# The last two attention heads: output-weight tiles and turned rows prepared at earlier steps, filling products taken weight tile by weight tile

## The chip, the core and the metric

The kernel runs on one core of a Trainium2 chip. The core has five engines, each with its own queue of instructions, which it works through in order: TensorE (PE; its weight loads are shown as PEld), VectorE (DVE), ScalarE (ACT), GpSimd (POOL) and SyncE (SP), which here issues all transfers. They meet only at semaphores. PE writes to PSUM, which has eight banks of 128 x 512 numbers; ACT and DVE read them.

The metric is the time of one execution on the device in microseconds (us). Three runs of the kernel before took 1289.68, 1290.79 and 1286.98 us; the median is 1289.68.

## What is computed

One decoder layer on 1024 tokens of width 1024, in float32. Only the first half matters here:

```python
h = rmsnorm(x, mix_pre_norm)
q_a, k_a, v_a, q_h, f_h, i_h, g_h = split(h @ w_in)
attn = dilated_mixture_attention(q_a, k_a, v_a)     # 8 heads of 64
attn = rmsnorm(attn, attn_out_norm)                  # 512 columns
rec = hgrn2_recurrence(q_h, f_h, i_h, g_h)           # 512 columns
mixed = concatenate([attn, rec]) @ w_out
x = x + rmsnorm(mixed, mix_post_norm)
x = x + rmsnorm(relu(rmsnorm(x, mlp_pre_norm) @ w_ff1)**2 @ w_ff2, mlp_post_norm)
```

The recurrence `rec` is ready before the attention begins, so its part of the product with `w_out` can be made while the attention runs. The attention norm is one factor per token, so it can be applied to the product afterwards.

## The kernel before

**Precision.** Every operand of a large product is split into a high and a low part: ACT copies it to the rounded format (L83), DVE takes the remainder (L84). A product is then three matmuls, high x high, low x high and high x low (`three_pass`, L87 to L89). With 512 columns that is one *unit* in what follows: one 128-row slice of weights times one token tile.

**The order is written by hand.** The instructions stand on each engine in the order in which the program records them. Two devices shape it. `queue` holds generators that emit filling work in small pieces, and `fill(ns)` lets them emit until the pieces' nominal costs have used up the given budget (a piece of 650 is one unit); a generator that yields `None` is not ready and ends the filling. `drain()` empties the queue.

**The attention loop** has 64 steps, `s = 8 * head + block`, each for 128 queries. Step `s` records: the exponentials of step s+1 on ACT (`expo`, L681); the scores of step s+2, two matmuls for each 512 keys (`score`, L667 and L668, into banks "s") with bias and maximum on DVE (L670); the transposes of its own exponentials (`turn`, L694), four to a bank "t", split by ACT (L697) and DVE (L698); for each pair of blocks the products with the values (`weigh`, L711, copied by ACT to `ot`, L714), whose result is turned back a step later (`finish`, L722), reduced by DVE (L726) and multiplied by POOL (L727). Then come the hooks of the step, and then `fill`.

Each kind of bank has two buffers: "mm", "s", "t" and "pv". A matmul that begins a new block in a bank waits until the readers of the block before last of that kind are done.

**Filling work.** Up to step 44 the filling is the projection of the last pair of heads (`attn_proj(3)`). Its last product, the second half of the keys, lies in an "mm" bank until `keys_off` reads it: DVE scales it into `kf` (L563), ACT (L565) and POOL (L566) split it, and four transfers copy the parts to the other half of the partitions. For this half the call is put off (`put_off`) to a later step.

After that the filling is `early_out(t)`, t = 0 to 3: the product of the recurrence columns of token tile t with the first four 128-row tiles of `w_out`, in two halves of 512 output columns (banks `pwe`), copied by ACT to `esum`. That is 32 units. What it needs:

- the four weight tiles, `w_get(WO0 + j, 0)`, j = 0 to 3: load on SP (L104) into one of two buffers `raw`, split by ACT and DVE to `wh`/`wl` (two rotating buffers) or to tiles `woh`/`wol` elsewhere, as `WO_TAG` says. The next load is recorded with the split that frees its buffer. `w_get` does nothing for a tile that is split already;
- the rows: `row_rec(t)` multiplies them by a gain on POOL (L772), `row_turn(t, 0)` transposes them on PE (L812, a bank "t", `pmt`) and splits them with ACT and DVE to `emt`.

The last four weight tiles are split at steps 61 to 63 and after the loop, where also the attention rows are turned (`row_turn(t, 1)`) and the rest of the product (`late_out`, banks `pwo`) begins.

Of the kernel before, what the change touches and what calls it, by code (L numbers as in the profile page):

```python
# [11 lines left out]
AF = mybir.ActivationFunctionType  # L12
# [6 lines left out]
T = 1024  # L19
# [6 lines left out]
AH = 8  # L26
# [9 lines left out]
def hymba_layer(ctx, tc, x, w_in, w_out, w_ff1, w_ff2, g_pre, lb_logits, g_mix, g_post,  # L36
                g_mlp, g_mlp_post, bias_tab, level_masks, ident_in, fold_in, out):
    nc = tc.nc
    V, S, G, TE = nc.vector, nc.scalar, nc.gpsimd, nc.tensor
# [10 lines left out]
    def slab(tag, name, dtype=F32, shape=(P, T)):  # L50
        return sp.tile(list(shape), dtype, tag=tag, name=name,
                       bufs={"S": 9, "T": 9, "P": 3, "BT": 2, "V8": 2, "R": 1}[tag])

    def bank(tag, name):
        return ps.tile([P, 512], F32, tag=tag, name=name,
                       bufs={"mm": 2, "s": 2, "t": 2, "pv": 2}[tag])
# [25 lines left out]
    def split_into(hi, lo, src, eng=V):  # L82
        S.activation(hi, src, AF.Copy)  # L83
        eng.tensor_tensor(out=lo, in0=src, in1=f32(hi), op=ALU.subtract)  # L84

    def three_pass(dst, lhs, rhs, start, stop):
        TE.matmul(dst, lhs[0], rhs[0], start=start, stop=False)  # L87
        TE.matmul(dst, lhs[0], rhs[1], start=False, stop=False)  # L88
        TE.matmul(dst, lhs[1], rhs[0], start=False, stop=stop)  # L89
# [7 lines left out]
    parts = {}  # L97
    done = [0, 0]
# [8 lines left out]
    def w_split(eng=V):  # L107
        i = done[1]
        if i < len(stream):
            if done[0] <= i:  # L110
                w_load()
            hl = stream[i][1]
            if hl is None:
                hl = (wp.tile([P, T], F32R, tag="wh", name=f"wh{i}", bufs=2),
                      wp.tile([P, T], F32R, tag="wl", name=f"wl{i}", bufs=2))
            else:
                hl = hl()
            split_into(hl[0], hl[1], raws.pop(i), eng)
            parts[i] = hl
            done[1] += 1  # L120
            w_load()

    def w_get(i, ahead=1):
        while done[1] < min(i + 1 + ahead, len(stream)):
            w_split()
        return parts[i]
# [24 lines left out]
    for i in range(4 * HH, 4 * HH + 3 * (AH // 2)):  # L151
        stream.append((w_in[i], None))
    WO0 = len(stream)
    WO_TAG = (None, ("S", "S"), None, ("S", "BT"), ("S", "S"), ("S", "T"), ("T", "T"), ("T", "T"))

    def wo_dest(k, tags):
        return lambda: (slab(tags[0], f"woh{k}", F32R), slab(tags[1], f"wol{k}", F32R))

    for k, tags in enumerate(WO_TAG):
        stream.append((w_out[k * P:(k + 1) * P, :], tags and wo_dest(k, tags)))  # L160
# [6 lines left out]
    queue = []  # L167
    debt = [0.0]

    def fill(ns):  # L170
        debt[0] += ns
        while debt[0] > 0 and queue:
            try:
                cost = next(queue[0])
            except StopIteration:
                queue.pop(0)
                continue
            if cost is None:
                break
            debt[0] -= cost  # L180
        debt[0] = min(debt[0], 0.0)

    def drain():
        while queue:
            n = len(queue)
            fill(1e9)
            assert len(queue) < n or not queue
# [456 lines left out]
    def load_bias(hd):  # L644
        if hd < AH and hd not in bts:
            bts[hd] = slab("BT", f"bt{hd}") if hd < AH - 1 else early["table"][:, 0]
            nc.sync.dma_start(out=bts[hd], in_=bias_tab[hd])
# [86 lines left out]
    rows, xress, mts, pmo, gains, scales = {}, {}, {}, {}, {}, {}  # L734
    AL = (AH // 2 - 1) * P

    def load_gain(name, tag, src):
        gains[name] = slab(tag, name)
        nc.sync.dma_start(out=gains[name], in_=src.partition_broadcast(P))

    NE = 4
# [14 lines left out]
    def early_sums():  # L756
        early["sum"] = [wide.tile([P, 2, D], F32, tag="A", name=f"esum{q}") for q in range(NE // 2)]

    def early_sum(t):
        return early["sum"][t // 2][:, t % 2]  # L760

    def row_load(t):
        row = rows[t] = slab("S", f"row{t}")
        c = AW if t < NE else 0
        nc.sync.dma_start(out=row[:, c:AW + AL], in_=mix_dram[t * P:(t + 1) * P, c:AW + AL])

    def rec_row(t):
        return early["rows"][:, t] if t < NE else rows[t][:, :AW]

    def row_rec(t):  # L770
        gain = gains["early"] if t < NE else gains["gmix"][:, :AW]
        G.tensor_tensor(out=rec_row(t), in0=rec_row(t), in1=gain, op=ALU.mult)  # L772
# [27 lines left out]
    def row_turn(t, which, late=False):  # L800

        if t < NE and which == 0:
            dst = early["mt"][t // 2][:, t % 2]
        else:
            if (t, 1) not in mts and (t, 0) not in mts or t < NE:
                mts[t] = slab("V8", f"mt{t}", F32R, (P, 2, 2, 4, P))
            dst = mts[t][:, which]
        mts[t, which] = dst
        src = rec_row(t) if which == 0 else rows[t][:, AW:]
        pt = bank("pv" if late else "t", f"pmt{t}_{which}")  # L810
        for j in range(4):
            TE.transpose(pt[:, j * P:(j + 1) * P], src[:, j * P:(j + 1) * P], ident)  # L812
        split_into(dst[:, 0], dst[:, 1], pt.rearrange("p (j c) -> p j c", j=4))

    def out_mm(t, hf, which, pm, start, stop):
        mt = mts[t, which]
        sl = slice(hf * 512, hf * 512 + 512)
        for j in range(4):
            n = 4 * which + j
            while n >= done[1] - WO0:  # L820
                yield None
            wh, wl = parts[WO0 + n]
            three_pass(pm, (mt[:, 0, j], mt[:, 1, j]), (wh[:, sl], wl[:, sl]), start and j == 0, stop and j == 3)
            yield 650.0

    def early_out(t):
        for hf in range(2):
            pm = bank("mm", f"pwe{t}_{hf}")
            yield from out_mm(t, hf, 0, pm, True, True)
            S.activation(early_sum(t)[:, hf * 512:hf * 512 + 512], pm, AF.Copy)  # L830
            yield 0.0

    def late_out(t, hf):
        pm = pmo[t, hf] = bank("s" if t % 2 else "mm", f"pwo{t}_{hf}")
# [80 lines left out]
    def look(s):  # L915
        if s < len(steps):
            scored[s] = score(*steps[s])

    def raise_(s):
        if s < len(steps):  # L920
            exped[s] = expo(*steps[s], *scored.pop(s))
# [11 lines left out]
    for h in range(HH):  # L933
# [5 lines left out]
        if not last:  # L939
            drain()  # L940

    hooks = {
        45: lambda: [row_rec(0), row_rec(1)],
        46: lambda: [w_get(WO0, 0), row_rec(2), row_rec(3)],
        47: lambda: [row_turn(0, 0), w_get(WO0 + 1, 0), load_bias(AH - 1)],
        48: lambda: [drain(), load_gain("gmix", "R", g_mix), early_sums(), w_get(WO0 + 2, 0), row_turn(1, 0),
                     queue.extend(early_out(t) for t in range(NE))],
        49: lambda: [w_get(WO0 + 3, 0), row_turn(2, 0)],
        50: lambda: row_turn(3, 0),
        55: lambda: [row_load(t) for t in range(3)],  # L950
        59: lambda: [row_norm(0), row_gain(0)],
        60: lambda: [row_norm(1), row_gain(1)],
# [4 lines left out]
    n_steps = len(steps)  # L957
    to_weigh, to_fold = [], []
    for s in range(n_steps):
        if s % 16 == 6:  # L960
            first_done[s // 16] = True
        hd, b = steps[s]
        ready, to_weigh = to_weigh, []
        raise_(s + 1)
        fresh = (s + 2) % 16 == 0
        if not fresh:
            look(s + 2)
        turn(hd, b, exped.pop(s))
        if b % 2:
            to_weigh.append((hd, b // 2))  # L970
        to_fold, last_fold = [(i, g, weigh(i, g)) for i, g in ready], to_fold
        if fresh and s + 2 < n_steps:
            while pairs[(s + 2) // 16] is None:
                fill(1.0)
            if (s + 2) // 16 + 1 < AH // 2:
                drain()
                queue.append(attn_proj((s + 2) // 16 + 1))
            look(s + 2)
        for i, g, a in last_fold:
            finish(i, g, *a)  # L980
        hooks.get(s, lambda: None)()
        if b in (7, 0, 1):
            while put_off:
                keys_off(*put_off.pop())
        fill(3400.0 - 360.0 * b if s < n_steps - 20 else 1000.0 if s < n_steps - 16 else 1300.0)
    for i, g, a in to_fold:
        finish(i, g, *a)
    to_fold = [(i, g, weigh(i, g)) for i, g in to_weigh]
# [343 lines left out]
    def early_mm(q, p):  # L1332
        if p == 1:
            lay[q] = {"X": small.get(f"x{q}")}
            mm1(q, 1, "a", True)
            out_p1(q)
        else:
            mm1(q, 2, "a", False)
            early_out(q)
# [38 lines left out]
    large.add("A")  # L1378
    w1_load(2)
    early_out(4)  # L1380
    b_split("T2", h12)
    for q in range(2):
# [310 lines left out]
    for t in range(NT):  # L1693
# [3 lines left out]
        for j, c in enumerate(pieces):  # L1697
            pm = banks.get(f"fe{t}{j}")
# [21 lines left out]
    t, pieces, rf = late  # L1720
# [71 lines left out]
```

## Time and profile before

| | |
|---|---|
| median of three runs | 1289.68 us |
| the profiled execution | 1289.73 us |
| its span, first to last instruction | 1287.9 us |
| mean granted PE clock | 0.991 |
| attention steps 45 to 63, PE | about 500 to 567 us |
| `late_out` and the residual | about 571 to 660 us |
| DMA, mean over the span | 120 GB/s |

In the rows of a timeline the first number is the start in us from the beginning of the span, the second the duration of one instruction (or of a group of like ones), then engine, line, operation, output<-inputs and shape. A bracket at the end gives the idle time of the engine before the row and what ended it. Names are without their numbers: `pt` is the bank of transposes, `p` the exponentials, `pmt` the turned rows, `pwe` the filling products. Matmuls are pipelined: start to start is shorter than the duration of one.

### The profile page before, as it was taken

What the parts mean: (1) busy time and instruction counts of PE and PEld (TensorE: products, weight loads), DVE (VectorE), ACT (ScalarE), POOL (GpSimd) and SP (SyncE); (2) the same over time, 40 slices, a digit from 0 to 9 for tenths busy, and PEclk for the clock granted to TensorE, in tenths of its full rate; (3) what the DMA queues carried; (4) which work ended last, traced back from release to release, by engine and by line L of the source; (5) the groups of instructions that cost most, each with busy time, mean ns of one, the idle gap of its engine ahead of it and who ended that gap; (6) DMA issues with size and microseconds to landing.
All of it is one profiled execution on the core that took longest, in us unless ns stands there. A gap on an engine that the chain in (4) does not pass through costs nothing. (4 is left out here: it accounts for less than half of the span.)

```text
span 1287.9 us, 17288 instructions
## 1 busy us (share of the span) xinstructions
PE 1247.8 (97%) x6524; PEld 1061.3 (82%) x6524; DVE 885.1 (69%) x1524; ACT 533.3 (41%) x967; POOL 297.8 (23%) x308
## 2 busy tenths in 40 slices
PE   8999999999999998999999899999999999999997
PEld 8898989888888887887877788888878888888886
DVE  5686868675666666667658766666676776688956
ACT  6623232213555556564555322222235533344412
POOL 0000000012122223043250487575541000000012
PEclk9999999999999999898999999999999999999999
DMA  5201111123222323335242344443369454434423
GB/s 205 67 17 50 34 50 33 34 82 88 61 83 66 83 66 110 98 114 179 94 152 90 139 173 177 148 180 131 139 245 353 161 196 131 160 102 131 155 76 129
DMA packets 58578, 153.98 MB, mean 120 GB/s; under 512 B 4992, under 2 KB 12928, under 8 KB 58240
## 3 DMA queue, kind: packets, MB, share of 16 engines
q1 hardware_dynamic: 58496, 152.89, 35.1%
q8 instruction: 51, 0.84, 0.3%
q14 instruction: 31, 0.25, 0.1%
HBM read 106.73 MB, written 39.85 MB: 114 GB/s over the span
## 5 line engine op out<-in xcount | busy, mean ns | idle before, releaser
L87 PE MATMUL f<-bh,ah 128*128 128x512 f32 x392 | 152.5, 389 | 0.0
L88 PE MATMUL f<-bl,ah 128*128 128x512 f32 x392 | 152.5, 389 | 0.0
L89 PE MATMUL f<-bh,al 128*128 128x512 f32 x392 | 152.5, 389 | 0.0
L84 DVE TENSOR_TENSOR al<-ar,ah 128x1024 fp32r<-128x1024 f32 x49 | 60.6, 1236 | 48.2 <-ACT ah L83 17.6
L87 PEld LDWEIGHTS f<-bh,ah 128*128 128x128 f32 x392 | 73.6, 188 | 15.4
L89 PEld LDWEIGHTS f<-bh,al 128*128 128x128 f32 x392 | 73.6, 188 | 15.3
L88 PEld LDWEIGHTS f<-bl,ah 128*128 128x128 f32 x392 | 73.6, 188 | 15.1
L83 ACT ACTIVATE ah<-ar 128x1024 fp32r<-128x1024 f32 x49 | 52.0, 1062 | 48.8 <-DMA ar<-actd 22.0
L1707 POOL TENSOR_SCALAR fp<-fss 128x1 f32<-128x1 f32 x8 | 3.5, 432 | 267.4 <-ACT fd L1704 267.4
L670 DVE CUSTOM_DVE_ANT_0 p<-ps,bt 128x512 f32<-128x512 f32 (+2 forms) x84 | 44.3, 552 | 25.0 <-PE ps L668 24.8
L697 ACT ACTIVATE pth<-pt 128x512 fp32r<-128x512 f32 (+2 forms) x96 | 43.3, 486 | 42.3 <-PE pt L694 40.6
L698 DVE TENSOR_TENSOR ptl<-pt,pth 128x512 fp32r<-128x512 f32 (+2 forms) x96 | 50.2, 551 | 15.3 <-ACT pth L697 15.2
L681 ACT ACTIVATE p<-p,nm 128x128 f32<-128x128 f32 (+3 forms) x64 | 49.5, 773 | 9.3 <-DVE nm L676 6.2
L727 POOL TENSOR_TENSOR anat<-anat,rd 128x128 f32<-128x128 f32 x32 | 14.6, 455 | 150.5 <-DVE anat L726 146.9
L79 POOL TENSOR_SCALAR ms<-hss 128x8 f32<-128x8 f32 x4 | 0.8, 197 | 206.3 <-DVE hss L538 206.3
L83 ACT ACTIVATE bh<-br 128x1024 fp32r<-128x1024 f32 x28 | 29.7, 1060 | 43.2 <-PE f L89 37.9
L694 PE MATMUL pt<-ident,p 128*128 128x128 f32 x288 | 42.9, 276 | 4.7 <-DVE ptl L698 4.7
L1221 POOL TENSOR_TENSOR e<-x,e 128x512 f32<-128x512 f32 x14 | 20.6, 1473 | 102.5 <-DVE x L1172 102.5
L84 DVE TENSOR_TENSOR wl<-raw,wh 128x1024 fp32r<-128x1024 f32 x23 | 31.4, 1365 | 18.3 <-ACT wh L83 18.0
L694 PEld LDWEIGHTS pt<-ident,p 128*128 128x128 f32 x288 | 33.5, 141 | 9.3 <-DVE ptl L698 6.8
L711 PE MATMUL pov<-pth,v 128*128 128x256 f32 (+1 forms) x160 | 40.6, 288 | 0.0
L1574 DVE TENSOR_TENSOR acc<-f,acc 128x512 f32<-128x512 f32 x52 | 33.8, 684 | 8.3 <-PE f L89 8.3
(1615 smaller groups left out, 3905.9 us busy)
## 6 DMA issues: line engine op xcount, KB each, us to landing
ar<-actd SPq DMA_DIRECT2D x49, 512.0 KB, 3.7
raw<-in_w_in_dram SPq DMA_DIRECT2D x28, 512.0 KB, 3.6
w1r<-in_w_ff_dram SPq DMA_DIRECT2D x14, 1024.0 KB, 6.6
br<-in_w_ff_dram SPq DMA_DIRECT2D x14, 1024.0 KB, 7.2
actd<-e SPq DMA_DIRECT2D x17, 768.0 KB, 4.1
actd<-e SPq DMA_DIRECT2D x11, 1024.0 KB, 4.0
xr<-in_x_dram SPq DMA_DIRECT2D x8, 512.0 KB, 9.5
raw<-in_w_out_dram SPq DMA_DIRECT2D x8, 512.0 KB, 3.6
```

Of the source, the lines that this page charges most:

```text
L83: S.activation(hi, src, AF.Copy)
L84: eng.tensor_tensor(out=lo, in0=src, in1=f32(hi), op=ALU.subtract)
L87: TE.matmul(dst, lhs[0], rhs[0], start=start, stop=False)
L88: TE.matmul(dst, lhs[0], rhs[1], start=False, stop=False)
L89: TE.matmul(dst, lhs[1], rhs[0], start=False, stop=stop)
L670: V.tensor_tensor_reduce(out=pe[:, k0:k0 + n], in0=pS[:, :n], in1=bts[hd][:, o:o + n], scale=1.0, scalar=-3.0e38, op0=ALU.add, op1=ALU.max ...
L681: S.activation(pe[:, :nk], pe[:, :nk], AF.Exp, bias=nm[:, b:b + 1], accum_out=dn[:, b:b + 1])
L694: TE.transpose(pt[:, j * P:(j + 1) * P], pe[:, jj * P:(jj + 1) * P], ident)
L697: S.activation(hi, src, AF.Copy)
L698: V.tensor_tensor(out=lo, in0=src, in1=f32(hi), op=ALU.subtract)
L711: TE.matmul(po[:, c0:256], vst, pt[j // 4][q][:, j % 4, c0:], start=j == 0 and q == 0, stop=j == nj - 1 and q == 1)
L1574: V.tensor_tensor(out=acc_at(p, i), in0=pm, in1=acc_at(p, i), op=ALU.add)
```

## The change

Three things are changed, for the pair of heads 6 and 7 only.

- The hooks of steps 43 to 50 are laid out anew. The gain products move from steps 45 and 46 to 43 and 44, the first two turned row blocks from 47 and 48 to 45 and 46, the other two from 49 and 50 to 48 and 49; the second weight tile from 47 to 45, the third from 48 to 47, the fourth from 49 to 48; the filling starts at step 46 in place of 48. The put-off second half of the keys goes from step 47 to 46. The second weight tile now takes the rotating buffers, the third takes the two tiles "S".
- `early_out` opens both halves' banks at once and goes through the weight tiles outside and the halves inside; it asks for a weight tile before each, and ACT's copies come with the last weight tile.
- The budgets of `fill` from step 44 on: 1300 at steps 44 to 47 (1000 before), and 2000 - 200 x block from step 48 on (1300 before).

```diff
-    WO_TAG = (None, ("S", "S"), None, ("S", "BT"), ("S", "S"), ("S", "T"), ("T", "T"), ("T", "T"))
+    WO_TAG = (None, None, ("S", "S"), ("S", "BT"), ("S", "S"), ("S", "T"), ("T", "T"), ("T", "T"))
...
     def early_out(t):
-        for hf in range(2):
-            pm = bank("mm", f"pwe{t}_{hf}")
-            yield from out_mm(t, hf, 0, pm, True, True)
-            S.activation(early_sum(t)[:, hf * 512:hf * 512 + 512], pm, AF.Copy)
-            yield 0.0
+        pms = [bank("mm", f"pwe{t}_{hf}") for hf in range(2)]
+        for j in range(4):
+            while j >= done[1] - WO0:
+                yield None
+            for hf, pm in enumerate(pms):
+                sl = slice(hf * 512, hf * 512 + 512)
+                three_pass(pm, [mts[t, 0][:, i, j] for i in range(2)], [w[:, sl] for w in parts[WO0 + j]], j == 0, j == 3)
+                if j == 3:
+                    S.activation(early_sum(t)[:, sl], pm, AF.Copy)
+                yield 650.0
...
-        45: lambda: [row_rec(0), row_rec(1)],
-        46: lambda: [w_get(WO0, 0), row_rec(2), row_rec(3)],
-        47: lambda: [row_turn(0, 0), w_get(WO0 + 1, 0), load_bias(AH - 1)],
-        48: lambda: [drain(), load_gain("gmix", "R", g_mix), early_sums(), w_get(WO0 + 2, 0), row_turn(1, 0),
-                     queue.extend(early_out(t) for t in range(NE))],
-        49: lambda: [w_get(WO0 + 3, 0), row_turn(2, 0)],
-        50: lambda: row_turn(3, 0),
+        43: lambda: [row_rec(0), row_rec(1)],
+        44: lambda: [row_rec(2), row_rec(3), w_get(WO0, 0)],
+        45: lambda: [drain(), w_get(WO0 + 1, 0), row_turn(0, 0)],
+        46: lambda: [early_sums(), row_turn(1, 0), queue.extend(early_out(t) for t in range(NE))],
+        47: lambda: [w_get(WO0 + 2, 0), load_bias(AH - 1)],
+        48: lambda: [load_gain("gmix", "R", g_mix), w_get(WO0 + 3, 0), row_turn(2, 0)],
+        49: lambda: row_turn(3, 0),
...
-        if b in (7, 0, 1):
+        if b in (7, 0, 1) or s == 46:
             while put_off:
                 keys_off(*put_off.pop())
-        fill(3400.0 - 360.0 * b if s < n_steps - 20 else 1000.0 if s < n_steps - 16 else 1300.0)
+        fill(3400.0 - 360.0 * b if s < n_steps - 20 else 1300.0 if s < n_steps - 16 else 2000.0 - 200.0 * b)
```

## The prediction

> **What bounds the kernel now.** The page comes first: it says which engine sets the end.
>
> ```profile
> span 1287.9 us, 17288 instructions
> PE 1247.8 (97%) x6524; PEld 1061.3 (82%) x6524; DVE 885.1 (69%) x1524; ACT 533.3 (41%) x967; POOL 297.8 (23%) x308
> PE 43%; DVE 2%; issue 0%; ACT 0%; DVEq 0%; POOL 0%; POOLq 0%; ACTq 0%
> ```
>
> TensorE (PE) is busy 97% of the span and leads the chain that ended last. Its work does not change, so the change can only act on PE's waits and on its clock. Next I read PE's own timeline where the change acts, from step 45 (head 5, block 5) to step 50 (head 6, block 2). A bracket gives the idle time before the row and what ended it.
>
> ```profile
> 500.64 0.38 PE L722 MATMUL pov<-ident,ot 128*128 128x128 f32 x2
> 502.00 0.98 PE L694 MATMUL pt<-ident,p 128*128 128x128 f32 x7 [0.98 <-DVE ptl L698]
> 506.94 0.63 PE L812 MATMUL pmt<-ident,erows 128*128 128x128 f32 x4 [0.98 <-POOL erows L772]
> 510.41 0.40 PE L88 MATMUL pwe<-wl,emt 128*128 128x512 f32 x1
> 510.64 0.39 PE L89 MATMUL pwe<-wh,emt 128*128 128x512 f32 x1
> 513.49 0.44 PE L694 MATMUL pt<-ident,p 128*128 128x128 f32 x2 [1.32 <-DVE ptl L698]
> 516.29 0.63 PE L812 MATMUL pmt<-ident,erows 128*128 128x128 f32 x4 [2.14 <-issue]
> 518.89 0.80 PE L88 MATMUL pwe<-wol,emt 128*128 128x512 f32 x1 [0.87 <-DVE wol L84]
> 519.91 0.63 PE L667 MATMUL ps<-kh,q 128*128 128x512 f32 x1
> ```
>
> The five waits sum to 6.29 us. Three are waits for one of the two "t" banks, which is free again only when ACT has copied the block of transposes in it and DVE has taken the remainder (the row at 516.29, "issue", is one of them: its bank held the turned block before). One is put down to POOL's gain products, one to a split weight tile. Then the clock, in stretches of 3.413 us counted from 517.52 (the columns are length, then busy PE, PEld, DVE, ACT, POOL, then the granted clock):
>
> ```profile
> 510.69:514.11 3.42, 2.10 (x11) 1.31 (x9) 1.30 (x6) 3.02 (x7) 2.29 (x2) 1.00 0.75 225
> 514.11:517.52 3.41, 1.27 (x9) 1.07 (x8) 3.12 (x8) 3.08 (x8) 0.25 (x1) 1.00 1.08 294
> 517.52:520.93 3.41, 2.54 (x8) 1.66 (x6) 1.91 (x3) 0.73 (x3) 1.24 (x1) 0.50 0.96 336
> 520.93:524.35 3.42, 3.42 (x17) 3.23 (x16) 1.87 (x8) 1.62 (x4) 0.00 (x0) 0.50 0.68 226
> 524.35:527.76 3.41, 3.41 (x21) 2.94 (x20) 2.43 (x7) 2.26 (x5) 0.00 (x0) 1.00 0.00 1
> 596.03:599.44 3.41, 1.47 (x10) 0.86 (x8) 1.95 (x2) 2.60 (x9) 1.67 (x5) 1.00 1.01 338
> 599.44:602.85 3.41, 2.63 (x6) 2.10 (x7) 2.65 (x5) 1.22 (x4) 2.18 (x4) 0.50 0.17 67
> 602.85:606.27 3.42, 3.42 (x9) 2.64 (x9) 3.31 (x5) 1.33 (x4) 0.00 (x0) 0.50 0.00 0
> ```
>
> On this grid every stretch has a clean 1.00 or 0.50. A stretch in which PE was busy 1.27 or 1.47 us (idle 2.14, 1.94) is followed by half clock; one with 2.10 is not. Half clock lasts one stretch more when PE was not busy enough in the first (2.54, 2.63). So an idle share of over about half costs up to 3.4 us. The first dip costs (6.83 - 0.87)/2 = 3.0 us, and the early waits together some 9 us. That is all that can be won here.
>
> **The change, part by part.** *What is as before.* Same matmuls, copies and transfers. The first output tile was already split while the last key product ran, so its call at step 44 issues nothing. The four gain products go past one POOL instruction only; their rows have landed by then, and 5.00 us from about 495.1 end before the first is needed. The loads on SP move with the splits that free their buffers, ahead of the last key copies by one load. I cost this at nothing, because those copies are first read in step 50; with that cover gone it would be one issue.
>
> ```profile
> 503.11 5.00 POOL L772 TENSOR_TENSOR erows<-erows,etable 128x512 f32<-128x512 f32 x4
> 510.43 0.35 SPq L104 DMA_DIRECT2D raw<-in_w_out_dram  x1
> ```
>
> *The early stretch.* I carry each engine's list forward in the changed order; an instruction starts when its engine is free and its inputs are there, with these durations:
>
> ```profile
> 501.25 1.02 DVE L698 TENSOR_TENSOR ptl<-pt,pth 128x512 fp32r<-128x512 f32 x2
> 507.60 0.60 ACT L83 ACTIVATE emt<-pmt 128x512 fp32r<-128x512 f32 x1 [1.00 <-PE pmt L812]
> 508.10 1.05 ACT L83 ACTIVATE woh<-raw 128x1024 fp32r<-128x1024 f32 x1
> 508.24 0.69 DVE L84 TENSOR_TENSOR emt<-pmt,emt 128x512 fp32r<-128x512 f32 x1 [0.41 <-ACT emt L83]
> 509.18 1.23 DVE L84 TENSOR_TENSOR wol<-raw,woh 128x1024 fp32r<-128x1024 f32 x1 [0.25 <-ACT woh L83]
> 510.32 0.68 DVE L563 TENSOR_TENSOR kf<-pm_ak,rrow 128x512 f32<-128x512 f32 x1
> ```
>
> Until 500.8 nothing differs. The first turned block now takes the bank that frees at 502.0 (wait 1.2). Step 46's second block of transposes needs the bank of that turned block. But the second weight tile's split stands ahead of its split: DVE is free of ptl at 502.27 and of the 0.4 us reduction at 502.7, takes 1.2 for the weight and 0.7 for the rows, and PE goes on at 504.6, having stood still since 502.9 (1.64). Then products, second turned block, and the first unit (three matmuls of one weight tile and half: 3 x 0.23 = 0.69) at 506.9. The second half's bank, claimed at once now, is the one that holds the last key product. Its reader kf is queued on DVE behind the remainder of the second turned block, which waits for ACT until 507.7: 507.7 + 0.65 + 0.68 = 509.05, so PE waits from 507.6 to 509.1 (1.47). Behind it PE is dense until the fourth tile's remainder, DVE 516.5 + 1.23, holds it from 517.0 to 517.8 (0.8). Step 50's scores start at 521.75. So the waits are 5.1 us in place of 6.29: mostly moved, not filled.
>
> By then 10 units are done, against 4 by 519.91 before (the order of the instructions gives both counts).
>
> *To step 59.* As mark I take the turn of head 7's first pair of blocks, 551.29 below. Before, 31.38 us lie between step 50 and it, with 18 units; the change has 19. 31.38 - 0.38 (fourth turned block already done) - 2.2 (half of the 4.4 us at half clock) + 0.69 + 0.85 = 30.34, so the mark comes at 552.09, 0.8 later. The 0.85 are two bank waits in steps 54 to 56, where the smaller fills stand. One of them: below, the transposes are issued by 539.69 and their first bank is back at 540.08 + 0.69; a 0.14 us turn and 0.35 of scores now lie between instead of a further 1.4 of products, so 0.55 stay open; the other, by the same reading, is 0.3.
>
> ```profile
> 539.69 0.38 PE L722 MATMUL pov<-ident,ot 128*128 128x128 f32 x2
> 540.08 1.29 DVE L698 TENSOR_TENSOR ptl<-pt,pth 128x512 fp32r<-128x512 f32 x2 [0.45 <-ACT pth L697]
> ```
>
> *The late stretch.* Here 18 filling matmuls (4.1 us) go. Is that 4.1 us off the end?
>
> ```profile
> 551.29 0.38 PE L722 MATMUL pov<-ident,ot 128*128 128x128 f32 x2
> 559.62 0.63 PE L812 MATMUL pmt<-ident,row 128*128 128x128 f32 x4 [1.10 <-DVE ptl L698]
> 567.91 0.39 PE L711 MATMUL pov<-ptl,v 128*128 128x256 f32 x1
> 571.06 0.48 PE L87 MATMUL pwo<-woh,mt 128*128 128x512 f32 x1
> 553.72 0.31 ACT L784 ACTIVATE dm<-anat 128x128 f32<-128x128 f32 x1 [1.12 <-POOL anat L727]
> 565.91 0.58 ACT L830 ACTIVATE esum<-pwe 128x512 f32<-128x512 f32 x1
> 566.38 1.08 ACT L697 ACTIVATE pth<-pt 128x512 fp32r<-128x512 f32 x2
> 558.78 1.02 DVE L698 TENSOR_TENSOR ptl<-pt,pth 128x512 fp32r<-128x512 f32 x2
> 566.03 1.22 DVE L84 TENSOR_TENSOR wol<-raw,woh 128x1024 fp32r<-128x1024 f32 x1 [1.33 <-ACT woh L83]
> 567.18 1.28 DVE L698 TENSOR_TENSOR ptl<-pt,pth 128x512 fp32r<-128x512 f32 x2
> ```
>
> No. From 553.72 ACT works through its list almost without a break, and DVE follows it: PE starts at 559.62 when ptl (558.78 + 0.69) gives a bank back, and at 567.91 when ptl (567.18 + 0.69) is there, which stood behind a weight split that waited for ACT. The filling lay in waits that ACT sets. What is more, one esum copy (0.47 from start to start) moves ahead of the exponentials of this stretch. So the late products start at 571.06 + 0.8 + 0.5 = 572.35: 1.3 later at full clock. Bounds: -4.1 if PE set this stretch, +0.5 as worked out; the rows are with ACT. The same bookkeeping on the order of before gives 571.15 for the row at 571.06.
>
> *The clock.* Early: idle from 500.8 to 502.0 and from 502.9 to 504.6, 2.8 of 3.8 us. On the recorded grid the stretch 500.45 to 503.87 has 2.1 idle, more than the 1.94 that halved the clock. Half clock to 510.69, with the 1.47 wait partly absorbed, puts step 50 at 524.0: +2.25 (bounds 0 and 3.4). Late: the waits are now 2.5, 1.2, 0.9, 1.1 and 1.2 us between 558.6 and 569, bare of filling; wherever the grid lies, some stretch has over 1.9 idle. One stretch at half clock costs 1.6 (bounds 0 and 3.4).
>
> The Trainium skill (TensorE: Matmul & The Clock Gate, section "HAM oscillation — how this bites in real kernels") has the abstract rule that PE should show no idle gaps over about 3.4 us. By it the change would lose no clock, since its longest gap is 2.5 us, and the sum would be 1291.0. The trace here disagrees: gaps of 2.14 us and less have halved the clock twice.
>
> *Sum.* The profiled execution took 1289.73 (span 1287.9 and 1.8 around it; the median of the runs is 1289.68). 1289.73 + 1.3 + 2.25 + 1.6 = 1294.9, against the median 1294.8.
>
> **The rivals.** *The clock stays full*, because the grid lies so that both waits are cut in two: 1291.0. For: a stretch with 1.32 idle passed. Against: the late waits are too many. 0.10. *The dip at 599.44 falls away*, since the wait before it shifts on the grid by 5 us and is cut in two: it costs (6.83 - 0.78)/2 = 3.0, so 1291.8. 0.18. *The late half clock holds two stretches* and reaches into the late products, which are dense: 1.7 to 3.4 more, 1297.5. 0.12. *Faster: PE, not ACT, sets the late stretch.* If ACT and DVE come to the mark ahead, the 18 matmuls gone are time won: 0.8 - 4.1 = -3.3 with no idle and so no late dip, and with the early waits cut by the grid: 1286.4. It decides if ACT reaches the row of 553.72 with no wait; it waited 1.12. 0.06.
>
> **How the numbers follow.** The forecast, 1294.8, has 0.54. About 0.3%, 3.9 us, can be told from no change: under 1285.8 is faster, over 1293.6 slower. Of the last rival two thirds are faster: 0.04. The first two, the rest of the last and 0.10 of the forecast's own spread (1292.5 to 1297, some of it under the bound) make 0.40 for the same; the other 0.44 and the third rival make 0.56 for slower. The range, 1288.5 to 1298.0, leaves out the faster rival and the top of the third.
>
> **What would show it.** In the changed profile: a wait of about 1.6 us for emt's remainder before a seven-block turn near 504.5, one of about 1.5 at the first pwe of the second half with kf as releaser, the scores of step 50 no earlier than 521.7, half clock soon after 504, five bare waits from 558 to 570, late products at 572 or later. The forecast is wrong if the late stretch shrinks by more than 2 us, or if the early idle time is under 3 us.

## The result and the profile after

| | before | after |
|---|---|---|
| median of 20 runs | 1289.74 us | 1294.30 us |
| lowest and highest | 1286.73 to 1292.24 | 1290.80 to 1297.21 |
| ratio, 95% interval | | 1.0036 [1.0027, 1.0045] |
| the profiled execution | 1289.73 us | 1293.01 us |

The change costs 4.6 us, against a forecast of 5.1. The page's first rows after:

```profile
span 1291.2 us, 17292 instructions
PE 1249.0 (97%) x6524; PEld 1062.0 (82%) x6524; DVE 885.0 (69%) x1524; ACT 533.3 (41%) x967; POOL 298.5 (23%) x308
PE 43%; DVE 2%; issue 0%; ACT 0%; DVEq 0%; POOL 0%; POOLq 0%; ACTq 0%
```

The same 6524 matmuls, and PE still leads the chain. The time therefore went into PE's waits and clock. Part of the difference between these two spans lies at the very start, ahead of anything the change touches; the first rows of PE's timeline before and after:

```profile
2.26 5.74 PE L279 MATMUL pig<-warm 128*128 128x256 f32 x18 [2.26 <-ACT warm L205]
```

```profile
2.26 6.84 PE L279 MATMUL pig<-warm 128*128 128x256 f32 x18 [2.26 <-ACT warm L205]
```

The same 18 opening matmuls took 1.10 us longer, nearly all of the 1.2 us that PE's busy time grew by. So I compare from a common row: PE's first wait of the stretch, which ended at 502.00 before and at 503.12 after. PE's timeline after, rows with a wait and the marks used in the prediction:

```profile
503.12 0.63 PE L812 MATMUL pmt<-ident,erows 128*128 128x128 f32 x4 [1.02 <-issue]
505.53 0.55 PE L694 MATMUL pt<-ident,p 128*128 128x128 f32 x3 [1.34 <-DVE emt L84]
511.69 0.50 PE L87 MATMUL pwe<-wh,emt 128*128 128x512 f32 x1 [1.30 <-DVE kf L563]
520.42 0.50 PE L88 MATMUL pwe<-wol,emt 128*128 128x512 f32 x1 [0.67 <-DVE wol L84]
524.40 0.39 PE L667 MATMUL ps<-kh,q 128*128 128x512 f32 x1
...
543.12 0.33 PE L694 MATMUL pt<-ident,p 128*128 128x128 f32 x1 [0.41 <-DVE ptl L698]
554.85 0.38 PE L722 MATMUL pov<-ident,ot 128*128 128x128 f32 x2
563.66 0.68 PE L812 MATMUL pmt<-ident,row 128*128 128x128 f32 x4 [2.23 <-DVE ptl L698]
565.75 0.90 PE L694 MATMUL pt<-ident,p 128*128 128x128 f32 x3 [0.56 <-DVE mt L84]
571.21 0.38 PE L711 MATMUL pov<-pth,v 128*128 128x256 f32 x1 [1.56 <-ACT pth L697]
572.59 0.39 PE L711 MATMUL pov<-ptl,v 128*128 128x256 f32 x1 [0.99 <-DVE ptl L698]
575.11 0.44 PE L722 MATMUL pov<-ident,ot 128*128 128x128 f32 x2 [0.53 <-ACT ot L714]
575.74 0.48 PE L87 MATMUL pwo<-woh,mt 128*128 128x512 f32 x1
```

All four early waits are where the forecast put them, with the releasers that it named: the bank (1.02; the profile names no releaser here, only "issue"), the turned rows' remainder (1.34), the scaled keys kf (1.30), the fourth weight tile's remainder (0.67). The late stretch has five bare waits, together 5.87 us. From the common row to the first late product (the last row) PE took 72.62 us; before, 571.06 - 502.00 = 69.06. That is 3.56 us more. PE was idle for 9.71 us of this stretch, against 7.05 before, so 2.7 of the 3.56 are idle time, and it has changed place: up to the turn of 554.85 (551.29 before) it fell from 5.3 to 3.8 us, and behind it it rose from 1.7 to 5.9, by 4.1 us, the time of the 18 matmuls that no longer stand behind the turned rows. The clock after, in stretches of the grid (length, busy PE, PEld, DVE, ACT, POOL, granted clock):

```profile
502.67:506.08 3.41, 1.61 (x13) 1.41 (x14) 2.85 (x7) 3.06 (x5) 1.31 (x1) 1.00 0.01 2
506.08:509.50 3.42, 3.42 (x19) 3.42 (x18) 1.70 (x6) 0.87 (x2) 0.00 (x0) 0.50 0.40 151
560.70:564.11 3.41, 1.18 (x11) 0.98 (x10) 2.56 (x9) 2.37 (x7) 2.32 (x5) 1.00 0.00 0
564.11:567.50 3.39, 2.83 (x14) 2.43 (x13) 2.04 (x3) 3.12 (x6) 0.40 (x1) 0.50 0.02 5
601.66:605.07 3.41, 1.39 (x9) 1.15 (x10) 2.08 (x3) 2.60 (x9) 1.54 (x6) 1.00 0.84 290
605.07:608.48 3.41, 3.41 (x9) 2.44 (x8) 3.38 (x6) 0.11 (x1) 1.56 (x2) 0.50 0.00 0
```

Stretches with 1.61, 1.18 and 1.39 us of work are each followed by one at half clock. The first two such pairs lie on the new bare waits, early and late. The third is an old one, but it lasts one stretch where before it lasted two. In this pair of runs the clock does not make the difference: between the common row and the late products half clock takes (3.42 + 2.83)/2 = 3.1 us after and (2.54 + 3.42)/2 = 3.0 before, and between 100 and 1280 us the run before has five stretches at half clock, the run after four.

### The profile page after: what moved, and what is told of

The parts are those of the page before. It is cut to its first block, busy times and chain, and to the rows that moved or that the text cites. A ratio compares the mean times of both kernels' runs of the same rounds, so it can differ in the third digit from the quotient of the medians.

```text
span 1291.2 us, 17292 instructions
## 1 busy us (share of the span) xinstructions
PE 1249.0 (97%) x6524; PEld 1062.0 (82%) x6524; DVE 885.0 (69%) x1524; ACT 533.3 (41%) x967; POOL 298.5 (23%) x308
## 5 line engine op out<-in xcount | busy, mean ns | idle before, releaser
L711 PE MATMUL pov<-ptl,v 128*128 128x256 f32 (+1 forms) x160 | 38.8, 288 | 1.0 <-DVE ptl L698 1.0
```

The source lines that it names most:

```text
L711: TE.matmul(po[:, c0:256], vst, pt[j // 4][q][:, j % 4, c0:], start=j == 0 and q == 0, stop=j == nj - 1 and q == 1)
```

## The experiments

The question was which of the three edits costs the time, and whether it is PE's idle time, the clock, or ACT's chain. Each kernel was timed in five rounds beside the kernel before (medians 1289.95, 1289.92, 1289.71 and 1289.49 us in the four groups, 14 to 35 runs). The one traced run of a kernel need not lie at its median: it took 1294.74 us for `drop18` (median 1292.62), 1290.53 for `hold4` (1287.71), 1288.76 for `late_hold` (1286.05) and 1285.01 for `late_kept` (1287.09). So waits are read from the traces, and what a change is worth from the medians. "Late units" counts the filling units that PE's order has behind the turned attention rows of step 61, that is, in the late waits.

| kernel | late units | median us | ratio to before, 95% interval |
|---|---|---|---|
| before | 6 | 1289.7 | |
| after | 0 | 1294.3 | 1.0036 [1.0027, 1.0045] |
| `budget_old` | 2 | 1291.67 | 1.0015 [1.0006, 1.0024] |
| `before_budget` | 3 | 1293.22 | 1.0023 [1.0015, 1.0032] |
| `drop18` | 0 | 1292.62 | 1.0020 [1.0011, 1.0029] |
| `spare18` | 0 | 1295.42 | 1.0039 [1.0026, 1.0051] |
| `late_kept` | 6 | 1287.09 | 0.9976 [0.9967, 0.9985] |
| `hold4` | 6 | 1287.71 | 0.9987 [0.9978, 0.9995] |
| `spare_all` | 0 | 1292.13 | 1.0014 [1.0004, 1.0024] |
| `both` | 0 | 1294.40 | 1.0033 [1.0022, 1.0044] |
| `late_hold` | 6 | 1286.05 | 0.9972 [0.9962, 0.9982] |
| `late_hold3` | 6 | 1286.13 | 0.9969 [0.9957, 0.9982] |
| `late_turn` | 6 | 1285.00 | 0.9966 [0.9955, 0.9977] |

**The budgets alone.** `budget_old` is the changed kernel with the budgets of before, `before_budget` the reverse.

```diff
-        fill(... 1300.0 if s < n_steps - 16 else 2000.0 - 200.0 * b)
+        fill(... 1000.0 if s < n_steps - 16 else 1300.0)
```

> The changed kernel with the fill budgets of the kernel before (1000 at steps 44 to 47, 1300 from step 48); everything else as changed. Theory A (ACT and DVE set the late stretch, and the larger early budgets strip it of its cover): the late waits shrink from 5 us in sum to under 3, the late products start about 2.6 us earlier at full clock, and a late half-clock stretch becomes unlikely (another 1 to 1.6): 1289.5 to 1291, ratio to before 0.999 to 1.001. Rival B (the earlier preparation and the order of the products cost the time, the budgets nothing): stays at 1293 to 1295, ratio 1.003 to 1.004.

> The kernel before with only the fill budgets of the change. Theory A: up to four units stand at step 48, before their weight tiles are split, so the early waits change their place (about 2.7 us for the third tile near 512 to 514), and six or fewer units are left for steps 59 to 63, so part of the late stretch is bare: late products 0.5 to 1 us later, with some chance of a late half clock: 1290 to 1292, ratio 1.000 to 1.002. Rival B (budgets do nothing): ratio 1.000. If budgets alone were the whole loss of the change: 1294.

Undoing the budgets in the changed kernel gives back 2.6 us of 4.6 (1294.3 to 1291.67), a little less than theory A expected (1289.5 to 1291). Putting them into the kernel before costs 3.3 us, more than the 1290 to 1292 expected. Neither kernel keeps the late units of before. In `budget_old` the filling starts two steps sooner and has used up four more by then. Its early waits are the changed kernel's (1.02, 1.34, 1.31, 0.70). PE's timeline of `budget_old` late:

```profile
559.76 0.63 PE L812 MATMUL pmt<-ident,row 128*128 128x128 f32 x4 [1.07 <-DVE ptl L698]
565.34 1.12 PE L694 MATMUL pt<-ident,p 128*128 128x128 f32 x8 [1.43 <-DVE ptl L698]
567.49 0.39 PE L711 MATMUL pov<-pth,v 128*128 128x256 f32 x1 [0.81 <-ACT pth L697]
568.86 0.39 PE L711 MATMUL pov<-ptl,v 128*128 128x256 f32 x1 [0.99 <-DVE ptl L698]
571.96 0.69 PE L722 MATMUL pov<-ident,ot 128*128 128x128 f32 x2 [0.53 <-ACT ot L714]
```

The two units left shorten the first wait from 2.23 to 1.07, but all five together only fall from 5.87 to 4.83, not under 3.

In `before_budget` the price lies at the other end. Its late waits are 2.90 us in all, with no half clock there. But its filling stands ahead of a weight tile that is not split yet:

```profile
514.75 0.78 PE L87 MATMUL pwe<-wh,emt 128*128 128x512 f32 x1 [2.66 <-ACT wh L83]
```

Behind this wait the clock was half for three stretches (514.80 to 525.04), where the profiled run before had two. So the count of late units alone does not give the time.

**Work left out.** `drop18` is the kernel before without its last six filling units (18 matmuls): of the last token tile's recurrence product only two of eight units are made.

```diff
-            yield from out_mm(t, hf, 0, pm, True, True)
+            if t < 3:
+                yield from out_mm(t, hf, 0, pm, True, True)
...
+            elif hf == 0:
+                for j in range(2):
...
```

> The kernel before without its last six filling units (18 matmuls; the product of the last early token tile lacks them), all copies and splits in place. Theory A: the 18 matmuls lay in waits that ACT and DVE set, so the late products start 0 to 0.6 us later than before, never earlier, the waits of PE after 558 grow by about 4 us in sum, and a half-clock stretch follows near 561 to 568: 1290 to 1292.5. Rival C (PE sets the late stretch): 4.1 us less, 1285.6.

Eighteen matmuls less made the kernel 2.7 us slower (1289.95 to 1292.62), just over the top of what theory A expected. The waits from 558 on grew by 4.35 us (1.63 before, 5.98 here), for 4.1 us of work left out. That refutes PE as what sets the late stretch, and more: the idle time has a price of its own. Stretches of the grid in `drop18`:

```profile
564.33:567.74 3.41, 1.54 (x11) 1.24 (x11) 1.94 (x4) 3.41 (x10) 1.44 (x4) 1.00 0.37 145
567.74:571.15 3.41, 2.46 (x11) 2.24 (x11) 3.23 (x6) 1.18 (x2) 3.02 (x3) 0.50 0.51 142
571.15:574.57 3.42, 2.89 (x14) 2.70 (x13) 0.74 (x1) 1.42 (x3) 0.08 (x1) 0.50 0.66 222
574.57:577.98 3.41, 3.41 (x9) 2.64 (x9) 1.42 (x3) 0.51 (x1) 0.40 (x1) 0.50 0.57 156
```

ACT was busy in all 3.41 us of the first stretch and PE in 1.54. Three stretches at half clock followed, the last of them on the dense late products.

**Work that nobody needs.** `spare18` puts 18 matmuls with an unread product into steps 61 to 63 of the changed kernel, behind the turned rows. `spare_all` puts 39 into the first two early waits and the late ones, nine of them ahead of those rows; the wait for kf stays (1.31 us).

```diff
+        if s >= 61:
...
+            for i in range(6):
+                TE.matmul(spare, mv[:, 0, i % 4], wv[0][:, :512], start=i == 0, stop=i == 5)
```

```diff
-        45: lambda: [drain(), w_get(WO0 + 1, 0), row_turn(0, 0)],
+        45: lambda: [drain(), spare(6), w_get(WO0 + 1, 0), row_turn(0, 0), spare(6)],
...
-        61: lambda: [row_turn(0, 1), w_get(WO0 + 4, 0)],
+        61: lambda: [spare(9), row_turn(0, 1), w_get(WO0 + 4, 0)],
...
+        if s >= 61:
+            spare(6)
```

> The changed kernel with 18 more matmuls of 512 columns, six at each of steps 61 to 63, whose result nobody reads. Theory A: they lie in the bare waits of the late stretch, so they cost nothing at full clock; and PE is busy enough there that no half clock follows near 564: 1 to 2 us less than the changed kernel, 1292.3 to 1293.3. Rival C (PE sets the late stretch): 4.1 us more, 1298.4. If the clock plays no part: 1294.3.

> The changed kernel with matmuls whose product nobody reads, in all its longer waits: six on each side of the first turned rows at step 45, nine ahead of the turned attention rows at step 61 and six each at steps 61 to 63 (39 more, some 9 us of work of PE). Theory A (the half clock behind the bare waits is what the changed kernel loses beside the moved filling; work that nobody needs keeps the clock as well as filling does): no half clock between 500 and 575, a granted clock of at least 0.995, 1290 to 1292.5. Rival B (the clock follows something else, or the matmuls do not fit into the waits): 1294.3 or more, up to 1298 if half of them lie on the path. In between, 1292.5 to 1294, both effects are there and cancel.

`spare18` missed its expectation: 1295.42, 1.1 us over the changed kernel in place of 1 to 2 below. PE's timeline shows why:

```profile
560.92 0.63 PE L812 MATMUL pmt<-ident,row 128*128 128x128 f32 x4 [2.23 <-DVE ptl L698]
573.33 0.44 PE L722 MATMUL pov<-ident,ot 128*128 128x128 f32 x2 [0.53 <-ACT ot L714]
```

Behind the turned rows the waits are gone but for 0.53. The longest, 2.23, stands ahead of the spare matmuls, and in this run the half clock still came right behind it, after a stretch with 1.19 us of work:

```profile
558.09:561.50 3.41, 1.19 (x11) 0.98 (x10) 2.55 (x9) 2.23 (x5) 2.33 (x5) 1.00 0.00 0
561.50:564.92 3.42, 3.42 (x13) 2.72 (x12) 1.92 (x2) 2.67 (x4) 0.40 (x1) 0.50 0.02 5
```

The late waits are 2.76 us in place of 5.87, so 3.1 of the 4.1 us of added work lay in waits and about 1 did not. That fits the 1.1, but five runs between 1293.40 and 1297.62 can't tell so small a difference from none. `spare_all` met the expectation of the clock theory: 39 matmuls more, some 9 us of PE's work, and 2.2 us faster than the changed kernel. Stretches of its trace:

```profile
502.70:506.10 3.40, 3.40 (x23) 2.90 (x23) 2.67 (x6) 2.85 (x5) 1.31 (x1) 1.00 0.05 18
557.00:576.00 19.00, 18.22 (x111) 15.33 (x110) 12.78 (x26) 13.95 (x32) 9.23 (x16) 1.00 0.28 93
```

PE is busy almost throughout, and the clock is full in both stretches where the changed kernel lost it. This is the clearest evidence that the idle time is charged twice, as a wait and as clock.

**The early order.** `both` records the turned rows ahead of the second weight split at step 45, and the readers of the last key product ahead of the hooks at step 46.

```diff
-        45: lambda: [drain(), w_get(WO0 + 1, 0), row_turn(0, 0)],
+        45: lambda: [drain(), row_turn(0, 0), w_get(WO0 + 1, 0)],
...
-        hooks.get(s, lambda: None)()
...
+        hooks.get(s, lambda: None)()
```

> The changed kernel with two places of its early order changed back: the first turned rows are recorded ahead of the split of the second weight tile at step 45, and at step 46 the readers of the last key product ahead of the step's own preparation. Theory A (the early waits are one chain of banks and only change place; what is lost lies in the budgets): the early waits are 1.2, 1.2, 0.8, 0.4, 1.3 and 0.8 us, together as before within 0.6 us, and the time is that of the changed kernel within 1 us, 1293.3 to 1295.3. Rival B (the order of the early preparation is the cost, the two waits of 1.3 us for the remainder of the rows and for the scaled keys being new): 1291 to 1292.8.

1294.40, the time of the changed kernel. The early waits became 1.02, 0.97, 1.03 and 0.69 us, four where six were expected and 0.6 less in all; the one for kf is gone. So they change place, and these two places of the order are not the cost. No run takes back the new order of the products (weight tile by weight tile) by itself, but `late_kept`, the next, has it and is faster than the kernel before.

**The late units given back.** `late_kept` is the changed kernel with other budgets alone, so that two units are left for each of the steps 61 to 63.

```diff
-        fill(... 1300.0 if s < n_steps - 16 else 2000.0 - 200.0 * b)
+        fill(... 650.0 if s in (52, 54, 56, 58) else 1300.0)
```

> The changed kernel with smaller filling budgets, so that two units are left for each of the steps 61 to 63 (1300 at every step from 44 on, 650 at steps 52, 54, 56 and 58). Theory A (the loss behind step 59 comes from the bare waits, whose clock it also halves; filling left over for them gives it back): carried forward by the rows of the profile before, the first late product comes 4 to 5 us sooner behind the mark of step 47 than the changed kernel's 72.6 us, so 68 to 69 us, and the time is 1286 to 1290, below both kernels. Rival B (the early waits and their half clock decide, the late part gives back what it gets): 1292 to 1295. Rival C (the place of filling is worth nothing, since only the number of stretches at half clock counts): within 1 us of the changed kernel, 1293.5 to 1295.

1287.09: 7.2 us under the changed kernel and 2.8 under the kernel before. PE's timeline of `late_kept`:

```profile
501.96 0.63 PE L812 MATMUL pmt<-ident,erows 128*128 128x128 f32 x4 [1.02 <-issue]
504.37 0.55 PE L694 MATMUL pt<-ident,p 128*128 128x128 f32 x3 [1.34 <-DVE emt L84]
508.98 0.50 PE L87 MATMUL pwe<-wh,emt 128*128 128x512 f32 x1 [1.31 <-DVE kf L563]
518.40 0.63 PE L812 MATMUL pmt<-ident,erows 128*128 128x128 f32 x4 [0.70 <-DVE emt L84]
546.40 0.38 PE L722 MATMUL pov<-ident,ot 128*128 128x128 f32 x2
555.22 0.63 PE L812 MATMUL pmt<-ident,row 128*128 128x128 f32 x4 [1.55 <-DVE ptl L698]
566.03 0.44 PE L722 MATMUL pov<-ident,ot 128*128 128x128 f32 x2 [0.53 <-ACT ot L714]
566.66 0.48 PE L87 MATMUL pwo<-woh,mt 128*128 128x512 f32 x1
```

The late waits are 1.55 and 0.53 in place of five. From the first wait to the late products it is 64.70 us against 72.62, 7.9 sooner. This run had no half clock there at all; without the 3.1 us that it took in the changed kernel's run, 4.8 remain, within the 4 to 5 expected. At the turn of 546.40 this kernel and the one before (551.29) have both done 22 units. From the first wait that took 44.44 us here and 49.29 before. Of the 4.85 us, 1.9 are early waits (4.37 in place of 6.29), and 3.0 are the half clock that the profiled run before had there. With as many late units as before, the medians still differ by 2.8. So the preparation itself, made sooner, is a gain; the filling that it let PE use up early is what cost.

**Filling held back for the early waits.** `hold4` is the kernel before with four units of the last key projection kept from steps 42 and 43 for 45 and 46. `late_hold` does the same to `late_kept`, two units on each side of the turned rows. `late_hold3` leaves one unit more for step 61, ahead of its turned rows. The diff is that of `late_hold` against the changed kernel.

```diff
-        45: lambda: [drain(), w_get(WO0 + 1, 0), row_turn(0, 0)],
+        45: lambda: [fill(1300.0), w_get(WO0 + 1, 0), row_turn(0, 0), drain()],
...
-        fill(3400.0 - 360.0 * b if s < n_steps - 20 ...
+        fill(3400.0 - 360.0 * b - (1300.0 if s in (42, 43) else 0.0) if s < n_steps - 20 ...
```

> The kernel before with 1300 less of filling at steps 42 and 43 and 1300 in place of 1000 at steps 44 to 47, so that four units of the last key projection are left for steps 45 and 46, where PE waited 0.98 us at 502.00 and again at 506.94. The hooks and the late part are those of before. Theory A (filling that lies on a wait gives back that wait and the clock behind it): 1287.5 to 1289.3, 1 to 2 us below the kernel before, and the wait at 502 gone. Rival B (those units held the earlier steps dense, and their waits only come sooner): 1289.5 to 1291, with new waits between 490 and 500. Rival C (the grid of the clock decides, not one wait): the same as before within its own spread of 1288 to 1292, with stretches at half clock at other places than before.

> The kernel of the run late_kept (the changed preparation, two units left for each of the steps 61 to 63), with four units of the last key projection held back from steps 42 and 43 to step 45, half of them ahead of the first turned rows and half behind. Theory A (filling that lies on a wait gives back the wait and the clock behind it): the two early waits of 1.02 and 1.34 us vanish, those for the scaled keys (about 1.3) and for the remainder of the fourth weight tile or rows (0.7) stay, the late ones are as in late_kept; late_kept's median of 1287.1 less 2.4 us of waits gives 1284.7, range 1283.5 to 1286. Rival B (the held units open waits in steps 42 to 45 in their place): 1286.5 to 1288. Rival C (the two changes act on the same half clock, so that nothing is won twice): 1286 to 1287.

> The kernel of the run late_hold with one unit more left for step 61 (650 in place of 1300 at step 50 too), recorded ahead of that step's turned attention rows, where late_kept still waited 1.55 us. Theory A: the wait becomes 0.8 us and the time 0.7 us less than that of late_hold, 1283 to 1285.3. Rival B (the chain of ACT sets the late stretch, so that the wait moves behind the unit without getting shorter): the same as late_hold within 0.4 us.

`hold4` came out as expected, 1287.71, with the wait at 502 gone; those of 0.98, 1.32 and 2.14 us are still there (0.81, 1.34, 2.15), and a short one of 0.29 came at 495.19. `late_hold` gained 1.0 in place of 2.4, and as its interval overlaps that of `late_kept`, even the 1.0 is not clear of the noise. PE's timeline, and then ACT's and DVE's, of `late_hold`:

```profile
506.42 0.53 PE L694 MATMUL pt<-ident,p 128*128 128x128 f32 x3 [2.43 <-DVE emt L84]
```

```profile
503.36 1.06 ACT L83 ACTIVATE wh<-raw 128x1024 fp32r<-128x1024 f32 x1 [2.55 <-PE pm_ak L88]
```

```profile
504.45 1.23 DVE L84 TENSOR_TENSOR wl<-raw,wh 128x1024 fp32r<-128x1024 f32 x1 [2.47 <-ACT wh L83]
505.59 0.68 DVE L84 TENSOR_TENSOR emt<-pmt,emt 128x512 fp32r<-128x512 f32 x1
```

The first early wait is gone, and the second has grown from 1.34 to 2.43. The weight split writes a rotating buffer from which PE was still reading the held units' weights (`pm_ak`). ACT stood behind that for 2.55 us, and DVE behind ACT, with the turned rows in both queues after the split. I had carried forward what each instruction reads, but not whose old contents it overwrites. In `late_hold3` the wait before the late turned rows fell from 1.59 to 0.86 as forecast, but the time is that of `late_hold` (1286.13 against 1286.05, seven and twelve runs); whether 0.7 us was won can't be told from these runs.

**The split behind the turned rows.** `late_turn` is `late_hold3` with the split last in step 45.

```diff
-        45: lambda: [fill(1300.0), w_get(WO0 + 1, 0), row_turn(0, 0), drain()],
+        45: lambda: [fill(1300.0), row_turn(0, 0), drain(), w_get(WO0 + 1, 0)],
```

> The kernel of the run late_hold3 with the first turned rows recorded ahead of the split of the second weight tile at step 45, and all held units ahead of that split. In late_hold3 PE waited 2.43 us for the remainder of the turned rows, which stood on DVE behind that split, and the split waited on ACT until PE had read the held units' weights out of the same rotating buffers. Theory A (that chain is the whole of what late_hold lost): the wait of 2.43 us goes, at most 0.5 us of it comes back at the second turned rows, the half clock behind it comes in fewer runs; 1286.1 less 2 gives 1284, range 1283 to 1285.2. Rival B (the split, now later on ACT, holds the exponentials and with them the transposes of step 46): a wait of 1 us or more between 505 and 510 in place of the one removed, 1285.5 to 1287.

PE's timeline of `late_turn`:

```profile
505.75 0.63 PE L812 MATMUL pmt<-ident,erows 128*128 128x128 f32 x4 [1.00 <-DVE ptl L698]
508.38 0.80 PE L87 MATMUL pwe<-wh,emt 128*128 128x512 f32 x1 [1.31 <-DVE kf L563]
```

The wait of 2.43 is gone, and 1.00 of it, rather than 0.5, stands at the second turned rows: part of the rival holds too. At 1285.00 this has the lowest median of the study, 4.5 us under the kernel before and 9.3 under the changed one, with the same matmuls. Its interval overlaps those of `late_kept`, `late_hold` and `late_hold3`, so how much of the last steps is gain stays open.

## Why the prediction was right

*What bounds the kernel.* Right: apart from the opening and the dip near 600, which the change does not touch, PE's waits and clock in the two stretches are what moved, and filling them otherwise moved the time both ways (1285.0 to 1295.4).

*The early waits.* Right in place, order and releaser. Each is 0.1 to 0.3 us shorter than worked out (1.02, 1.34, 1.30, 0.67 against 1.2, 1.64, 1.47, 0.8), 4.33 in all in place of 5.1. The second stands ahead of the last three of its step's seven transposes, not ahead of all seven.

*Early half clock.* It came soon after 504, at 506.08 (504.96 on the origin of before). It lasted one stretch of 3.42 in which PE was fully busy: 1.7 us, where the forecast had two stretches (503.87 to 510.69) and, with part of it absorbed, 2.25. That it came there at all is in part luck. The forecast placed it on the grid of the run before, and the phase of the grid is another in each run: behind the same two waits of 1.02 and 1.34 us the clock fell in the profiled runs of this kernel and of `budget_old`, and stayed full in those of `spare18` and `late_kept`. The scores of step 50 came at 524.40 - 1.12 = 523.28, forecast 524.0.

*To step 59.* 30.45 us from step 50 to the mark (554.85 - 524.40), forecast 30.34. Of the two bank waits forecast there (0.55 and 0.3), one is in the trace, 0.41.

*The late stretch.* Its mechanism is confirmed by `drop18`: the 18 filling matmuls lay in waits that ACT's chain sets, so taking them out wins nothing. From the mark to the turned rows it is 8.81 us (563.66 - 554.85) against 8.33 before: 0.48 more, as worked out for the esum copy that moved ahead. Behind the rows it is only 0.64 more, although a half-clock stretch with 2.83 busy lies there, which alone would account for 1.4 (the term was 1.6). So the size was somewhat off: 20.89 us in all against 19.77, 1.1 more, where the two terms gave 2.1. The five waits are 5.87 us together, where 6.9 were forecast. And from the mark on seven units went, not the six (18 matmuls) of the forecast: ten lay there before and three after; six is the count behind the turned rows.

*Behind the late products.* The sum took this part as unchanged; it was 715.5 us (1291.2 - 575.74) against 716.8 (1287.9 - 571.06). The dip that stood at 599.44 before was one stretch shorter. That is half of the second rival, in this run.

*The sum.* For the profiled pair: 1.12 at the opening, 3.56 to the late products, -1.38 behind them, together 3.3, the difference of the spans. The terms gave 5.15, all of it ahead of the late products, so there they are 1.6 too high: 0.6 up to the mark, mostly the early clock, and 1.0 behind it. The median is nearer to the forecast (0.5 below it), and that nearness is partly luck, since it hangs on how much clock a run loses: of the 20 runs, four with a mean granted clock of 0.995 took 1290.8 to 1291.3, nine with 0.993 or 0.994 took 1292.95 to 1294.84, and seven with 0.990 to 0.992 took 1295.3 to 1297.2. The first group lies at the time of the rival in which the clock stays full (1291.0), but no trace of such a run was taken. In the runs of the kernel before the mean clock does not order the times in this way (in one group 0.994 took 1291.54 and 0.991 took 1289.45).

*The rule weighed against the trace.* The longest wait after is 2.23 us, and the clock fell behind it. Another section of the same page of the Trainium skill fits better (TensorE: Matmul & The Clock Gate, section "A second HAM failure mode: psum-queue depth-cycling"): short idle times between groups of matmuls that cycle through PSUM banks can be enough. Here they were.

*What the prediction did not see.* It did not ask what the early preparation is worth if the filling stays where it was. `late_kept` shows a gain of 2.8 us over the kernel before in that case; keeping no unit back turns it into the loss: from the one kernel to the other each of the six late units is worth 7.2 / 6 = 1.2 us on average, though its three matmuls take 0.69.

## What to carry to other kernels

Filling work is a stock: count how much of it is left when the last waits of a phase come, and set the budgets backward from there, since making it ready sooner only helps if it is not also used up sooner. Try to fill the longest bare wait first and from its front: in the trace of `spare18` matmuls behind it did not save the clock that the wait had already lost, though no run here changes this alone. And when filling is moved, look also at the buffers that it reads: it keeps them from whoever writes them next.

## What the runs showed of the hardware

The grid of the clock has the same pitch in every profiled run, some 3.41 us, but another phase in each. `late_kept` had the same early waits of 1.02 and 1.34 us as the kernel after, and in its profiled run they cost no clock. Its stretches there, on the grid of its own dip at 595.88:

```profile
500.33:503.74 3.41, 1.68 (x14) 1.23 (x12) 3.37 (x11) 2.93 (x5) 1.25 (x2) 1.00 0.00 0
503.74:507.16 3.42, 2.79 (x23) 2.75 (x24) 2.33 (x7) 2.14 (x6) 0.24 (x1) 1.00 0.52 153
507.16:510.57 3.41, 2.10 (x14) 1.53 (x13) 1.65 (x4) 2.00 (x4) 0.91 (x1) 1.00 0.00 0
```

A boundary cut the second wait (503.03 to 504.37) in two. PE was busy for 1.68 us in the first stretch, and the clock stayed. After, the whole second wait and 0.45 us of the first fell into one stretch with 1.61 busy, and the clock fell. The two stretches differ by 0.07 us of work, but there is no sharp bound of busy time between them. In `both` a stretch with more work than either was followed by half clock:

```profile
569.47:572.88 3.41, 1.77 (x12) 1.57 (x13) 3.27 (x6) 2.03 (x4) 3.02 (x4) 1.00 0.27 79
572.88:576.30 3.42, 2.88 (x14) 2.60 (x13) 1.68 (x2) 1.67 (x3) 0.94 (x1) 0.50 0.64 212
```

And in `spare18` one with 1.58 us (725.34 to 728.75) was not. On the grids of the thirteen profiled runs, from 100 to 1260 us, every stretch at full clock with under 1.5 us of busy PE was followed by half clock and none with over 1.8; between them it went both ways.

The runs of one program lie up to 6 us apart (1290.80 to 1297.21 after). That the phase of the grid decides where in this range a run falls is a reading and not shown, since each kernel has one trace. Nor is it shown that filled waits narrow the range: `late_turn` has 1284.53 to 1286.27, but `drop18`, with its waits bare, has only 1292.32 to 1294.74. The Trainium skill (TensorE: Matmul & The Clock Gate, section "What's actually happening") describes a window of 3413 ns that runs freely and doesn't restart with the kernel; the dips here agree: they last 3.42, 6.83 or 10.24 us and begin at another phase in each run. Eighteen needed matmuls left out of the kernel before cost 2.7 us, and 39 unread ones put into the changed kernel won 2.2.
